# Norm pieces of a finished expert group moved between the second-layer products, on three engines, in a hybrid RWKV and mixture-of-experts layer

## The chip, the cores and the metric

One core of a Trainium2 chip runs the whole layer. The metric is device time in microseconds of one execution. Before the change it was 4061.99 us, the median of three runs (4059.59 to 4078.86).

## What is computed

The input is x, 4096 tokens of 1024 channels, float32. A projection, a pooling mixer, an RWKV-7 recurrence and an output product give `h = LayerNorm(alpha*x + mix)`. Then comes the part that matters here, a two-level mixture of experts and a last norm:

```python
g_top_p, g_idx = lax.top_k(softmax(h @ router_group + b), 1)     # 1 of 4 groups
e_top_logit, e_idx = lax.top_k(logits of that group's 8 experts, 2)
hid = silu(h[tok] @ exp_gate[e]) * (h[tok] @ exp_up[e])          # 1024 -> 256, per expert
ffn[tok] += (hid @ exp_down[e]) * weight                         # 256 -> 1024
y = LayerNorm(alpha * h + ffn) * ln2_g + ln2_b
```

Each token goes to two experts of one group, so a token's sum is complete when its group's eight experts are done.

## The kernel before

Three phases come first (`phase_project`, `phase_rwkv`, `phase_out`); the change leaves them alone. `phase_out` also routes the tokens, writes them to `d_h`, alpha times them to the accumulator `d_acc`, and writes a table of tokens per expert. Experts are ranked by load inside ranked groups, and the r-th expert gets a fixed number of 64-row blocks, `GIVEN[r]`: 7 6 6 5 5 5 5 4, then 6 5 5 5 5 4 4 4, then 7 6 5 4 4 4 4 3, then 4 4 3 3 3 3 3 3. Rows are worked on in spans of 128. The groups have `GGIVEN` = 10, 9, 9, 6 tiles of 128 tokens to norm.

`phase_moe` runs the 32 experts in one unrolled loop with a manual schedule: every engine executes its instructions in the order in which the program emits them, so the place of a call in the text is its place in the queue. All products are float32 split into a high and a low part, three matmuls for each. In expert r:

- `listed` and `load` (L1203, L1228) are DMAs on SP: the token table, and the weights of coming experts into six staging halves `ws`.
- `split` (L1214) turns one staged half into high (ACT copy, L1225) and low (DVE subtraction, L1226). Six halves an expert: g0 g1 u0 u1 d0 d1.
- `hidden` (L1300) is the first layer: for f in 0, 1 the gate and the up product (24 matmuls each, into p_gu banks), then silu (ACT), times (DVE, sg), high part hh (ACT), low part hl (DVE). A dictionary `work` hangs other calls behind the products (f, "g") and (f, "u"), ahead of that f's silu.
- `down` (L1332) is the second layer. A column j is 128 rows by 512 outputs; it has two halves f of three matmuls into one p_y bank. ACT weighs the finished column into y (L1330), and after two columns POOL adds y into `d_acc` by an indirect DMA (`scatter`, L1261).
- Between the columns, `rows` (L1280) prepares the next expert: a turn is four transposes on PE into one m_pt bank (L1275), then ACT writes xh (L1291) and DVE xl (L1292), which frees the bank. After every second turn POOL gathers a coming span of tokens (`ahead`, L1247).
- In the order of before, three columns get their first half, and from then on each column's second half is followed by the first half of the column three places on.

`Norms` handles a finished group while the next group's experts run, in experts i = 1 to 7 of that group. `fetch` gathers one or two tiles of `d_acc` on POOL (L1422). One expert later `stats` runs on DVE behind (0, "g"): sums of each tile (L1378, L1379), then fifteen tiny instructions for the root (`root`, L1382). Behind (1, "g") `apply` makes two DVE passes over each tile (L1406, L1407), and behind (1, "u") `store` writes it out by an indirect DMA on POOL (L1443). The experts before the first finished group, and the first one or two of each group, carry none of this. The last group is normed behind the loop in pairs of tiles, with the root from ACT's log and exponential (`log_root`, L1399). Two loops behind that take overflowing experts and have no passes for these inputs. An indirect DMA keeps its dependence on the POOL DMA just ahead of it, and is freed by hand from those that touch other rows (L1254).

Of the kernel before, what the change touches and what calls it, by code (L numbers as in the profile page):

```python
# [6 lines left out]
F32 = mybir.dt.float32  # L7
# [6 lines left out]
D = 1024  # L14
# [1138 lines left out]
def phase_moe(tc, A, hrow, acc, tab, gtab, plan, out):  # L1153
# [14 lines left out]
    KM = max(GIVEN)  # L1168
    RW = 64 * KM
    with ExitStack() as ctx:  # L1170
        cst = ctx.enter_context(tc.tile_pool(name="m_c", bufs=1))
        wsp = [ctx.enter_context(tc.tile_pool(name=f"m_w{i}", bufs=1)) for i in range(3)]
        wst = ctx.enter_context(tc.tile_pool(name="m_ws", bufs=6))
        xp = ctx.enter_context(tc.tile_pool(name="m_x", bufs=1))
        hp = ctx.enter_context(tc.tile_pool(name="m_h", bufs=1))
        fp = ctx.enter_context(tc.tile_pool(name="m_f", bufs=4))
        sm = ctx.enter_context(tc.tile_pool(name="m_s", bufs=3))
        pg = ctx.enter_context(tc.tile_pool(name="m_pg", bufs=3, space=PSUM))
        py = ctx.enter_context(tc.tile_pool(name="m_py", bufs=3, space=PSUM))
        ptr = ctx.enter_context(tc.tile_pool(name="m_pt", bufs=2, space=PSUM))  # L1180

        manual = ctx.enter_context(ExitStack())
        manual.enter_context(tc.manual_schedule())
# [145 lines left out]

            nc.scalar.activation(y[:n, i * 512:i * 512 + 512], p[:n], AF.Copy, scale=ix[:n, 1:2].bitcast(F32))  # L1330

        def down(r, hid, nxt):  # L1332

            ps = {}
            sp = spans[r]
            hi, lo = W[r]["d"]
            ix = IX.pop(r)
            same = []

            def part(j, f):  # L1340
                b, n = divmod(j, 2)
                a0, a1 = sp[b]
                if f == 0:
                    ps[j] = py.tile([128, 512], F32, name="p_y")
                a, c = hid[f]
                for i, (x, w) in enumerate(((a, hi), (c, hi), (a, lo))):
                    nc.tensor.matmul(ps[j][:a1 - a0], lhsT=x[:, a0:a1], rhs=w[:, f, n * 512:n * 512 + 512],  # L1347
                                     start=f == 0 and i == 0, stop=f == NF - 1 and i == 2)

            J = 2 * len(sp)  # L1350
            left = 2 * len(spans[r + 1]) if r + 1 < NE else 0
            for j in range(3):
                if left:
                    next(nxt)
                    left -= 1
                part(j, 0)
            for j in range(J):
                part(j, 1)
                a0, a1 = sp[j // 2]
                if j % 2 == 0:  # L1360
                    y = hp.tile([128, D], F32, name="y", bufs=4)
                weigh(y, j % 2, ps.pop(j), ix[:, j // 2], a1 - a0)
                if j % 2:
                    same.append(scatter(ix[:, j // 2], y, a1 - a0, r // EG, same))
                if j + 3 < J:
                    part(j + 3, 0)
                for _ in range(-(-left // (J - j))):
                    next(nxt)
                    left -= 1
            for _ in nxt:  # L1370
                pass

        def mean_var(hs):
            st = sm.tile([128, 2, 2, 6], F32, name="f_st")
            mv = sm.tile([128, 2, 2], F32, name="f_mv")
            for i, h in enumerate(hs):
                for c in range(2):
                    nc.vector.bn_stats(st[:, i, c, :], h[:, c * 512:c * 512 + 512])  # L1378
                nc.vector.bn_aggr(mv[:, i, :], st[:, i])  # L1379
            return mv  # L1380

        def root(mv, n):  # L1382

            va = sm.tile([128, 2], F32, name="f_va")[:, :n]
            yi = sm.tile([128, 2], I32, name="f_yi")[:, :n]
            ra = sm.tile([128, 2], F32, name="f_ra")
            tm = sm.tile([128, 2], F32, name="f_tm")[:, :n]
            rs = ra[:, :n]
            nc.vector.tensor_scalar(va, mv[:, :n, 1], 1e-5, None, op0=OP.add)
            nc.vector.tensor_scalar(yi, va.bitcast(I32), 1, None, op0=OP.arith_shift_right)  # L1390
            nc.vector.tensor_scalar(rs.bitcast(I32), yi, -1.0, float(0x5f3759df), op0=OP.mult, op1=OP.add)
            for _ in range(3):
                nc.vector.tensor_tensor(tm, rs, rs, op=OP.mult)
                nc.vector.tensor_tensor(tm, tm, va, op=OP.mult)
                nc.vector.tensor_scalar(tm, tm, -0.5, 1.5, op0=OP.mult, op1=OP.add)
                nc.vector.tensor_tensor(rs, rs, tm, op=OP.mult)
            return ra

        def log_root(mv, n):  # L1399
            ra = sm.tile([128, 2], F32, name="f_ra")  # L1400
            nc.scalar.activation(ra[:, :n], mv[:, :n, 1], AF.Ln, bias=leps)
            nc.scalar.activation(ra[:, :n], ra[:, :n], AF.Exp, scale=-0.5)
            return ra

        def scale(h, mv, rs, i):
            nc.vector.scalar_tensor_tensor(h, h, mv[:, i, 0:1], g2, op0=OP.subtract, op1=OP.mult)  # L1406
            nc.vector.scalar_tensor_tensor(h, h, rs[:, i:i + 1], b2, op0=OP.mult, op1=OP.add)  # L1407

        class Norms:


            def __init__(self, g):
                self.g, self.b, self.got = g, 0, []
                gs = bass.ds(eng.value_load(orow[0:1, g, 1:2], min_val=0, max_val=NG - 1), 1)
                self.ig = sm.tile([128, max(GGIVEN)], I32, name="ig", bufs=2)
                eng.dma_start(self.ig[:, :GGIVEN[g]], tg[gs, :, :GGIVEN[g]].rearrange("g p a -> (g p) a"))

            def fetch(self, n):
                self.new = []
                for _ in range(n):  # L1420
                    h = fp.tile([128, D], F32, name="f_h")
                    ld = nc.gpsimd.indirect_dma_start(  # L1422
# [7 lines left out]
                    self.b += 1  # L1430

            def stats(self, rsqrt):
                if self.got:
                    self.mv = mean_var([h for h, _ in self.got])
                    self.rs = rsqrt(self.mv, len(self.got))

            def apply(self):
                for i, (h, b) in enumerate(self.got):
                    scale(h, self.mv, self.rs, i)

            def store(self):
# [7 lines left out]
                self.got = []  # L1449

        def share(n, k):

# [15 lines left out]
        for r in range(NE):  # L1468
            g, i = divmod(r, EG)
            listed(r + 3)  # L1470
            work = {(0, "g"): [lambda: split(r, "d", 0), lambda: split(r, "d", 1)],
                    (1, "g"): [lambda: split(r + 1, "g", 0), lambda: split(r + 1, "g", 1)],
                    (1, "u"): [lambda: split(r + 1, "u", 0)]}
            if r == 1:
                nc.scalar.dma_start(g2, bcast_row(A["ln2_g"], D))
                nc.scalar.dma_start(b2, bcast_row(A["ln2_b"], D))
                work[0, "u"] = [plan.caps]
            if r == 2:
                work[0, "u"] = [plan.rest]
            if g and i == 1:  # L1480
                norms = Norms(g - 1)
                parts = share(GGIVEN[g - 1], EG - 2) + [0]
            if g and i:
                norms.fetch(parts[i - 1])
# [5 lines left out]
            if norms:  # L1490
                norms.got, norms.new = norms.new, []
            load(r + 1, "d")
            load(r + 2, "gu")
            down(r, hid, rows(r + 1))
        norms = Norms(NG - 1)
        for n in share(GGIVEN[NG - 1], (GGIVEN[NG - 1] + 1) // 2) + [0]:
            norms.fetch(n)
            norms.stats(log_root)
            norms.apply()
            norms.store()  # L1500
            norms.got = norms.new
        manual.close()

        rrow = cst.tile([1, 128, 4], I32, name="rrow")
# [39 lines left out]
        n = nc.values_load(rrow[0:1, 0, 3:4], min_val=0, max_val=S // 128)  # L1544
        av = acc.rearrange("(q p) d -> q p d", p=128)
        ov = o.rearrange("(q p) d -> q p d", p=128)
        with tc.For_i(0, n) as i:
            h = fp.tile([128, D], F32, name="f_h")
            eng.dma_start(h, av[bass.ds(i, 1)].rearrange("q p d -> (q p) d"))
            mv = mean_var([h])  # L1550
            scale(h, mv, log_root(mv, 1), 0)
            eng.dma_start(ov[bass.ds(i, 1)].rearrange("q p d -> (q p) d"), h)


# [46 lines left out]
```

## Time and profile before, and how to read it

| | |
|---|---|
| median of three runs | 4061.99 us |
| the profiled execution, its own time | 4087.32 us |
| its span, first to last instruction | 4085.7 us |
| PE matmul busy | 3409.8 us (83%) |
| DVE busy | 2019.8 us (49%) |
| ACT busy | 1577.1 us (39%) |
| POOL busy | 1628.1 us (40%) |
| mean granted TensorE clock | 0.868 |
| HBM read, written | 324.90, 206.92 MB |

PE is TensorE's matmuls, PEld its weight loads, DVE VectorE, ACT ScalarE, POOL GpSimd, SP the queue of most DMAs. An idle time is put down to the instruction or transfer that ended it. DMA share is the mean busy share of 16 DMA engines. Busy shares are means over stages with different limits, so a stage is read by itself.

### The profile page before, as it was taken

Reading aid. Unit: us, or ns where it says so; the run is one execution under the profiler, and the core shown is the slowest. Engines: PE = TensorE matmul, PEld = TensorE weight load, DVE = VectorE, ACT = ScalarE, POOL = GpSimd, SP = SyncE. Lnnn points to the kernel's source line nnn. Section 1 sums busy time; section 2 is a strip of 40 time slices with the busy share of each in tenths; the row PEclk is TensorE's granted clock in tenths of the full one; section 3 lists DMA queues with packets and bytes.
Section 4 is the critical chain, followed back from the end, with each engine's and each line's share of the span. In section 5 each row is a group of like instructions: output and inputs, shape, how many; then the busy total and the mean of one; then the engine's idle time right before and its main releaser. Section 6 shows DMA issues by size and latency. Waiting matters only on the chain. (4 is left out here: it accounts for less than half of the span.)

```text
span 4085.7 us, 70444 instructions
## 1 busy us (share of the span) xinstructions
PE 3409.8 (83%) x27401; PEld 2825.9 (69%) x27401; DVE 2019.8 (49%) x4087; ACT 1577.1 (39%) x2672; POOL 1628.1 (40%) x2951
## 2 busy tenths in 40 slices
PE   7999999999668888878888868999668887777772
PEld 6878877777557777767776756777557776566652
DVE  3222222222447776767666635565544445455564
ACT  2222211111244545454545435565424443333432
POOL 3000120000177777777777731334322223222222
PEclk9999999999777878787878769999879998887876
DMA  7433333322223333333333325565357777677763
GB/s 245 173 137 151 147 129 129 116 99 85 80 58 84 71 84 72 78 73 81 77 73 80 68 70 194 140 154 142 85 149 188 197 199 208 184 190 209 214 194 92
DMA packets 509752, 531.20 MB, mean 130 GB/s; under 512 B 297854, under 2 KB 411688, under 8 KB 505321
## 3 DMA queue, kind: packets, MB, share of 16 engines
q1 hardware_dynamic: 445752, 367.94, 31.7%
q0 software_dynamic: 33920, 106.02, 10.8%
q10 hardware_dynamic: 29744, 52.73, 3.5%
q8 instruction: 216, 3.54, 0.4%
q14 instruction: 120, 0.98, 0.1%
HBM read 324.90 MB, written 206.92 MB: 130 GB/s over the span
## 5 line engine op out<-in xcount | busy, mean ns | idle before, releaser
L134 PE MATMUL acc<-xhi,wh 128*128 128x512 f32 x1408 | 565.9, 402 | 5.4 <-DVE zo L176 5.1
L135 PE MATMUL acc<-xlo,wh 128*128 128x512 f32 x1408 | 559.4, 397 | 0.0
L136 PE MATMUL acc<-xhi,wl 128*128 128x512 f32 x1408 | 559.3, 397 | 0.0
L491 POOL TENSOR_TENSOR db<-db,tmp 96x126 f32<-96x126 f32 (+22 forms) x992 | 449.8, 453 | 77.7
L489 POOL TENSOR_TENSOR tmp<-db,gi 96x126 f32<-96x126 f32 (+22 forms) x992 | 430.6, 434 | 77.7
L176 DVE SCALAR_TENSOR_TENSOR zo<-acc,omu,zm 128x512 f32<-128x512 f32 x160 | 120.0, 751 | 660.5 <-ACT zm L173 622.3
L173 ACT ACTIVATE zm<-acc,muc 128x512 f32<-128x512 f32 x160 | 110.1, 690 | 719.7 <-PE acc L136 718.4
L134 PEld LDWEIGHTS acc<-xhi,wh 128*128 128x128 f32 x1408 | 265.4, 189 | 72.0 <-DVE zo L176 5.4
L135 PEld LDWEIGHTS acc<-xlo,wh 128*128 128x128 f32 x1408 | 265.7, 189 | 66.4 <-issue 3.8
L136 PEld LDWEIGHTS acc<-xhi,wl 128*128 128x128 f32 x1408 | 265.5, 189 | 63.4
L174 POOL COPY carry<-zm 128x1 f32<-128x1 f32 x160 | 30.4, 191 | 664.4 <-ACT zm L173 664.4
L1275 PE MATMUL m_pt<-m_id,xg 128*128 128x128 f32 (+1 forms) x648 | 108.9, 300 | 198.1 <-DVE xl L1292 163.7
L1275 PEld LDWEIGHTS m_pt<-m_id,xg 128*128 128x128 f32 (+1 forms) x648 | 83.3, 160 | 236.5 <-DVE xl L1292 179.1
L1261 POOL DMA_INDIRECT d_acc<-y,ix x81 | 131.8, 1627 | 266.3 <-DMA d_acc<-y,ix 107.1
L1061 PE MATMUL o_ps<-owh,mh 128*128 128x512 f32 x512 | 212.4, 415 | 17.1 <-ACT owh L889 17.0
L1347 PE MATMUL p_y<-wh_d,hh 128*128 128x512 f32 (+1 forms) x324 | 169.4, 523 | 59.2 <-ACT y L1330 51.4
L1292 DVE TENSOR_TENSOR xl<-m_pt,xh 128x512 fp32r<-128x512 f32 (+1 forms) x162 | 99.3, 629 | 240.0 <-ACT xh L1291 213.8
L1247 POOL DMA_INDIRECT xg<-d_h,ix x81 | 78.3, 966 | 337.9 <-PE m_pt L1275 328.9
L1061 PE MATMUL o_ps<-owh,ml 128*128 128x512 f32 x512 | 207.1, 404 | 5.2 <-POOL ml L876 5.2
L1061 PE MATMUL o_ps<-owl,mh 128*128 128x512 f32 x512 | 205.3, 402 | 0.5 <-DVE owl L890 0.3
L445 DVE TENSOR_TENSOR g<-tr,mask 128x384 f32<-128x384 f32 x256 | 130.4, 550 | 142.9 <-PE tr L443 142.9
L443 PE MATMUL tr<-ar,kb 64*128 64x128 f32 x1536 | 178.9, 364 | 24.9 <-DVE kb L430 17.0
(352 smaller groups left out, 8802.7 us busy)
## 6 DMA issues: line engine op xcount, KB each, us to landing
d_rkv<-zo SPq DMA_DIRECT2D x144, 256.0 KB
ws<-in_exp_gate_dram SPq DMA_DIRECT2D x64, 512.0 KB
ws<-in_exp_up_dram SPq DMA_DIRECT2D x64, 512.0 KB
ws<-in_exp_down_dram SPq DMA_DIRECT2D x64, 512.0 KB
xq<-in_x_dram SPq DMA_DIRECT2D x32, 512.0 KB
d_xsp<-xhi ACTq DMA_DIRECT2D x8, 2048.0 KB
d_xsp<-xlo ACTq DMA_DIRECT2D x8, 2048.0 KB
xlo<-d_xsp SPq DMA_DIRECT2D x8, 2048.0 KB
```

Of the source, the lines that this page charges most:

```text
L134: nc.tensor.matmul(ps, lhsT=whi[i][:, k, :], rhs=xhi[:, k, :], start=k == 0, stop=False)
L135: nc.tensor.matmul(ps, lhsT=whi[i][:, k, :], rhs=xlo[:, k, :], start=False, stop=False)
L136: nc.tensor.matmul(ps, lhsT=wlo[i][:, k, :], rhs=xhi[:, k, :], start=False, stop=k == KD - 1)
L176: nc.vector.scalar_tensor_tensor(zo, ps, omu[:, ix:ix + 1], zm[:, :SEG], op0=OP.mult, op1=OP.add)
L443: nc.tensor.matmul(ps[h][:, p, :], lhsT=KB[hs, i, :], rhs=AR[hs, i, :], start=True, stop=True)
L445: nc.vector.tensor_tensor(G[:, h, c::NC, :], ps[h], masks[c % 2].unsqueeze(1).to_broadcast([128, 3, 128]), op=OP.mult)
L489: e.tensor_tensor(tm, Dh[:, :a, x:x + 1].to_broadcast([96, a, b]), G[:, x, x + 1:].unsqueeze(1).to_broadcast([96, a, b]), op=OP.mult)
L491: e.tensor_tensor(Dh[:, :a, x + 1:], Dh[:, :a, x + 1:], tm, op=OP.add)
L1061: nc.tensor.matmul(ps, lhsT=a[:, k, :], rhs=w[k][:, ns], start=k == 0 and i == 0, stop=k == KD - 1 and i == 2)
L1261: st = nc.gpsimd.indirect_dma_start(out=acc, out_offset=bass.IndirectOffsetOnAxis(ap=ix[:n, 0:1], axis=0), in_=y[:n], in_offset=None, boun ...
L1275: nc.tensor.transpose(pt[:, k, :n], xg[:n, (4 * i + k) * 128:(4 * i + k + 1) * 128], ident[:n, :n])
L1347: nc.tensor.matmul(ps[j][:a1 - a0], lhsT=x[:, a0:a1], rhs=w[:, f, n * 512:n * 512 + 512], start=f == 0 and i == 0, stop=f == NF - 1 and i ...
```

## The change

The pools of staging memory come first, p_y loses one PSUM bank and m_pt gains it. A norm pass is split in three: x * root - mean * root on ACT, times ln2_g on DVE, plus ln2_b on POOL. `stats` returns a list of small pieces, and `down` issues one of them around each half column from the third on, in the expert that fetched the tile; scale, product and store follow in the next expert's first layer. In `down` each column is now finished at once, and the turns stand ahead of the half columns, as early as they come. Three splits move a place ahead. The last group is normed tile by tile, with four tiles fetched up front.

```diff
+        wst = ctx.enter_context(tc.tile_pool(name="m_ws", bufs=6))
+        wsp = [ctx.enter_context(tc.tile_pool(name=f"m_w{i}", bufs=1)) for i in range(3)]
         cst = ctx.enter_context(tc.tile_pool(name="m_c", bufs=1))
-        wsp = [ctx.enter_context(tc.tile_pool(name=f"m_w{i}", bufs=1)) for i in range(3)]
-        wst = ctx.enter_context(tc.tile_pool(name="m_ws", bufs=6))
...
-        py = ctx.enter_context(tc.tile_pool(name="m_py", bufs=3, space=PSUM))
-        ptr = ctx.enter_context(tc.tile_pool(name="m_pt", bufs=2, space=PSUM))
+        py = ctx.enter_context(tc.tile_pool(name="m_py", bufs=2, space=PSUM))
+        ptr = ctx.enter_context(tc.tile_pool(name="m_pt", bufs=3, space=PSUM))
...
-        def down(r, hid, nxt):
+        def down(r, hid, nxt, extra):
...
+                if f == 0:
+                    return
+                if n == 0:
+                    y[b] = hp.tile([128, D], F32, name="y", bufs=4)
+                weigh(y[b], n, ps.pop(j), ix[:, b], a1 - a0)
+                if n:
+                    same.append(scatter(ix[:, b], y[b], a1 - a0, r // EG, same))
             J = 2 * len(sp)
+            todo = [(0, 0), (1, 0), (0, 1), (1, 1)] + [(j, f) for j in range(2, J) for f in range(NF)]
             left = 2 * len(spans[r + 1]) if r + 1 < NE else 0
-            for j in range(3):
-                if left:
+            extra = list(extra)
+            for i, (j, f) in enumerate(todo):
+                for _ in range(-(-left // max(1, len(todo) - 3 - i))):
                     next(nxt)
                     left -= 1
-                part(j, 0)
-            for j in range(J):
-                part(j, 1)
...
+                    if extra and i > 1:
+                        extra.pop(0)()
+                part(j, f)
+                if extra and i > 1:
+                    extra.pop(0)()
...
             def stats(self, rsqrt):
-                if self.got:
-                    self.mv = mean_var([h for h, _ in self.got])
-                    self.rs = rsqrt(self.mv, len(self.got))
+                self.got, self.new = self.new, []
...
+                def shift():
+                    nc.vector.scalar_tensor_tensor(mr[:, :n], mv[:, :n, 0], -1.0, ra[:, :n], op0=OP.mult, op1=OP.mult)
+                return ([lambda i=i, h=h: sums_of(i, h) for i, (h, _) in enumerate(self.got)]
+                        + rsqrt(mv, ra, n) + [shift])
+            def scale(self, only=None):
+                for i, (h, b) in enumerate(self.got):
+                    nc.scalar.activation(h, h, AF.Identity, bias=self.mr[:, i:i + 1], scale=self.ra[:, i:i + 1])
             def apply(self):
                 for i, (h, b) in enumerate(self.got):
-                    scale(h, self.mv, self.rs, i)
+                    nc.vector.tensor_tensor(h, h, g2, op=OP.mult)
             def store(self):
                 for h, b in self.got:
+                    nc.gpsimd.tensor_tensor(h, h, b2, op=OP.add)
                     st = nc.gpsimd.indirect_dma_start(
...
             work = {(0, "g"): [lambda: split(r, "d", 0), lambda: split(r, "d", 1)],
-                    (1, "g"): [lambda: split(r + 1, "g", 0), lambda: split(r + 1, "g", 1)],
-                    (1, "u"): [lambda: split(r + 1, "u", 0)]}
+                    (0, "u"): [lambda: split(r + 1, "g", 0)],
+                    (1, "g"): [lambda: split(r + 1, "g", 1), lambda: split(r + 1, "u", 0)],
+                    (1, "u"): [lambda: split(r + 1, "u", 1)]}
...
-                work[0, "g"].append(lambda: norms.stats(root))
-                work[1, "g"].append(norms.apply)
-                work[1, "u"].append(norms.store)
+                work[0, "g"] += [norms.scale, norms.apply]
+                work[0, "u"].append(norms.store)
             hid = hidden(r, work)
-            split(r + 1, "u", 1)
...
+            if g and i:
+                extra = norms.stats(root)
+            down(r, hid, rows(r + 1), extra)
         norms = Norms(NG - 1)
-        for n in share(GGIVEN[NG - 1], (GGIVEN[NG - 1] + 1) // 2) + [0]:
...
+        norms.fetch(min(4, GGIVEN[-1]))
+        every = norms.new
+        while every or norms.b < GGIVEN[-1]:
+            norms.new = every[:1]
+            every = every[1:]
+            for x in norms.stats(log_root):
+                x()
+            norms.scale()
+            norms.apply()
+            norms.store()
+            if norms.b < GGIVEN[-1]:
+                norms.fetch(1)
+                every += norms.new
```

The root's instructions are the same, cut into one opening piece of three and three steps of four; `log_root` is one piece. The overflow loop behind uses the same three passes.

## Rows read from the trace of the kernel before

**Rows 1.** Windows by stage: length, busy PE, PEld, DVE, ACT, POOL, clock, DMA share, GB/s.

```profile
2997.00:3323.90 326.90, 279.35 (x1553) 237.30 (x1553) 145.00 (x263) 146.28 (x219) 76.76 (x60) 0.97 0.69 183
3323.90:3531.10 207.20, 151.77 (x885) 129.99 (x883) 125.20 (x231) 80.43 (x123) 64.71 (x49) 0.86 0.72 203
3531.10:3805.60 274.50, 210.76 (x1154) 178.36 (x1153) 143.15 (x252) 104.66 (x157) 76.02 (x58) 0.82 0.70 192
3805.60:4023.90 218.30, 164.04 (x1073) 136.29 (x1071) 127.38 (x239) 87.03 (x137) 63.56 (x46) 0.85 0.67 183
```

**Rows 2.** Waits of the expert loop: who waited for whom, us, times, longest.

```profile
PE m_pt L1275 <- DVE xl L1292: 161.8, 31, 10.7
...
PE p_y L1347 <- ACT y L1330: 51.4, 66, 0.8
```

**Rows 3.** Windows of single experts, columns as in rows 1: 4, 7, 20, 21, 25, 27.

```profile
3148.30:3178.60 30.30, 26.28 (x158) 21.97 (x157) 12.49 (x16) 14.37 (x23) 7.48 (x7) 1.00 0.73 190
3238.00:3260.50 22.50, 20.15 (x146) 18.18 (x145) 12.06 (x15) 13.02 (x21) 7.18 (x5) 1.00 0.73 203
...
3682.50:3710.00 27.50, 20.55 (x137) 18.47 (x136) 17.44 (x34) 12.01 (x19) 7.70 (x8) 0.88 0.83 239
3710.00:3744.10 34.10, 22.85 (x137) 20.06 (x137) 21.68 (x39) 12.10 (x19) 10.30 (x8) 0.75 0.68 190
3827.20:3848.90 21.70, 19.33 (x138) 17.15 (x137) 10.83 (x14) 11.67 (x19) 6.13 (x6) 1.00 0.91 251
3877.70:3911.20 33.50, 22.04 (x138) 17.72 (x137) 20.64 (x39) 11.46 (x19) 10.05 (x8) 0.75 0.67 195
```

**Rows 4.** Timeline of PE in expert 4's second layer: start, us, instruction, idle before.

```profile
3166.47 0.66 PE L1275 MATMUL m_pt<-m_id,xg 128*128 128x128 f32 x4 [1.69 <-DVE xl L1292]
...
3167.90 0.39 PE L1347 MATMUL p_y<-wh_d,hl 128*128 128x512 f32 x1
3168.13 0.40 PE L1347 MATMUL p_y<-wl_d,hh 128*128 128x512 f32 x1
3169.30 0.50 PE L1347 MATMUL p_y<-wh_d,hh 128*128 128x512 f32 x1 [0.78 <-ACT y L1330]
```

**Rows 5.** Lines of the expert loop: group, count, busy us, mean ns, idle before.

```profile
L1226 DVE TENSOR_TENSOR wl_g<-ws,wh_g 128x1024 fp32r<-128x1024 f32 x62 | 73.2, 1222 | 15.1 <-ACT wh_g L1225 15.1
...
L1225 ACT ACTIVATE wh_g<-ws 128x1024 fp32r<-128x1024 f32 x62 | 61.8, 1044 | 0.0
...
L1406 DVE SCALAR_TENSOR_TENSOR f_h<-f_h,f_mv,g 128x1024 f32<-128x1024 f32 x28 | 35.8, 1279 | 0.0
```

**Rows 6.** Timeline in phase_out: a POOL subtraction and a DVE pass begun beside it.

```profile
2493.33 2.40 POOL L876 TENSOR_TENSOR ml<-m,mh 128x1024 fp32r<-128x1024 f32 x1 [9.29 <-ACT mh L875]
...
2493.84 2.97 DVE L1145 SCALAR_TENSOR_TENSOR h<-h,ln_mv,g 128x1024 f32<-128x1024 f32 x1
```

**Rows 7.** Timeline of POOL, experts 19 and 20: a second scatter, then the norm gather.

```profile
3688.57 1.59 POOL L1261 DMA_INDIRECT d_acc<-y,ix  x1 [5.24 <-DMA d_acc<-y,ix]
3696.01 1.22 POOL L1422 DMA_INDIRECT f_h<-d_acc,ig  x1 [5.85 <-DMA d_acc<-y,ix]
```

**Rows 8.** Timelines behind the loop: POOL's first gather and last store, DVE, ACT.

```profile
4034.46 0.99 POOL L1422 DMA_INDIRECT f_h<-d_acc,ig  x1 [2.29 <-DMA d_acc<-y,ix]
...
4038.91 1.28 DVE L1378 BATCH_NORM_STATS2 f_st<-f_h 128x6 f32<-128x512 f32 x2 [21.91 <-DMA f_h<-d_acc,ig]
4040.23 0.21 DVE L1379 BATCH_NORM_AGGREGATE f_mv<-f_st 128x2 f32<-128x12 f32 x1
...
4044.10 1.28 ACT L1402 ACT_TABLE_LOAD   x1
4045.39 0.20 ACT L1402 ACTIVATE f_ra<-f_ra 128x2 f32<-128x2 f32 x1
...
4074.01 0.98 POOL L1443 DMA_INDIRECT out_dram<-f_h,ig  x1 [3.11 <-DMA out_dram<-f_h,ig]
```

**Rows 9.** Timelines ahead of the loop: the last split of first weights, the first turn.

```profile
2965.41 1.06 ACT L1225 ACTIVATE wh_u<-ws 128x1024 fp32r<-128x1024 f32 x1 [0.71 <-DMA ws<-in_exp_up_dram]
...
2987.96 1.94 PE L1275 MATMUL m_pt<-m_id,xg 128*128 128x128 f32 x8 [34.48 <-DMA ws<-in_exp_up_dram]
```

More of the change, by code (lines that the diff above doesn't have):

```diff
@@ L1370, in down @@
             for _ in nxt:
                 pass
[L1373 to L1407, printed above, removed]
+            for x in extra:
+                x()
@@ L1432, in stats, with sums_of @@
             def stats(self, rsqrt):
-                if self.got:
-                    self.mv = mean_var([h for h, _ in self.got])
-                    self.rs = rsqrt(self.mv, len(self.got))
+                self.got, self.new = self.new, []
+                n = len(self.got)
+                if not n:
+                    return []
+                st = sm.tile([128, 2, 2, 6], F32, name="f_st")
+                mv = sm.tile([128, 2, 2], F32, name="f_mv")
+                ra = sm.tile([128, 2], F32, name="f_ra")
+                mr = sm.tile([128, 2], F32, name="f_mr")
+                self.ra, self.mr = ra, mr
+                def sums_of(i, h):
+                    for c in range(2):
+                        nc.vector.bn_stats(st[:, i, c, :], h[:, c * 512:c * 512 + 512])
+                    nc.vector.bn_aggr(mv[:, i, :], st[:, i])
+                def shift():
[5 more added lines that the diff above has]
+                    nc.scalar.activation(h, h, AF.Identity, bias=self.mr[:, i:i + 1], scale=self.ra[:, i:i + 1])
             def apply(self):
                 for i, (h, b) in enumerate(self.got):
-                    scale(h, self.mv, self.rs, i)
+                    nc.vector.tensor_tensor(h, h, g2, op=OP.mult)
             def store(self):
                 for h, b in self.got:
+                    nc.gpsimd.tensor_tensor(h, h, b2, op=OP.add)
                     st = nc.gpsimd.indirect_dma_start(
@@ L1449, in store, with root, begin, step @@
                 self.got = []
+        def root(mv, ra, n):
+            va = sm.tile([128, 2], F32, name="f_va")[:, :n]
+            yi = sm.tile([128, 2], I32, name="f_yi")[:, :n]
+            tm = sm.tile([128, 2], F32, name="f_tm")[:, :n]
+            rs = ra[:, :n]
+            def begin():
+                nc.vector.tensor_scalar(va, mv[:, :n, 1], 1e-5, None, op0=OP.add)
+                nc.vector.tensor_scalar(yi, va.bitcast(I32), 1, None, op0=OP.arith_shift_right)
+                nc.vector.tensor_scalar(rs.bitcast(I32), yi, -1.0, float(0x5f3759df), op0=OP.mult, op1=OP.add)
+            def step():
+                nc.vector.tensor_tensor(tm, rs, rs, op=OP.mult)
+                nc.vector.tensor_tensor(tm, tm, va, op=OP.mult)
+                nc.vector.tensor_scalar(tm, tm, -0.5, 1.5, op0=OP.mult, op1=OP.add)
+                nc.vector.tensor_tensor(rs, rs, tm, op=OP.mult)
+            return [begin, step, step, step]
+        def log_root(mv, ra, n):
+            def both():
+                nc.scalar.activation(ra[:, :n], mv[:, :n, 1], AF.Ln, bias=leps)
+                nc.scalar.activation(ra[:, :n], ra[:, :n], AF.Exp, scale=-0.5)
+            return [both]
         def share(n, k):
@@ L1476, in phase_moe @@
                 nc.scalar.dma_start(b2, bcast_row(A["ln2_b"], D))
-                work[0, "u"] = [plan.caps]
+                work[0, "u"].append(plan.caps)
             if r == 2:
[L1479 to L1482, printed above, removed]
+                work[0, "u"].append(plan.rest)
+            extra = []
             if g and i:
+                if i == 1:
+                    norms = Norms(g - 1)
+                    parts = share(GGIVEN[g - 1], EG - 2) + [0]
                 norms.fetch(parts[i - 1])
-                work[0, "g"].append(lambda: norms.stats(root))
-                work[1, "g"].append(norms.apply)
-                work[1, "u"].append(norms.store)
+                work[0, "g"] += [norms.scale, norms.apply]
+                work[0, "u"].append(norms.store)
             hid = hidden(r, work)
-            split(r + 1, "u", 1)
-            if norms:
-                norms.got, norms.new = norms.new, []
             load(r + 1, "d")
             load(r + 2, "gu")
-            down(r, hid, rows(r + 1))
+            if g and i:
+                extra = norms.stats(root)
+            down(r, hid, rows(r + 1), extra)
         norms = Norms(NG - 1)
-        for n in share(GGIVEN[NG - 1], (GGIVEN[NG - 1] + 1) // 2) + [0]:
-            norms.fetch(n)
-            norms.stats(log_root)
+        norms.fetch(min(4, GGIVEN[-1]))
[4 more added lines that the diff above has]
+            for x in norms.stats(log_root):
+                x()
+            norms.scale()
             norms.apply()
             norms.store()
-            norms.got = norms.new
+            if norms.b < GGIVEN[-1]:
+                norms.fetch(1)
+                every += norms.new
         manual.close()
@@ L1546, in phase_moe @@
         ov = o.rearrange("(q p) d -> q p d", p=128)
+        again = norms
         with tc.For_i(0, n) as i:
@@ L1549, in phase_moe @@
             eng.dma_start(h, av[bass.ds(i, 1)].rearrange("q p d -> (q p) d"))
-            mv = mean_var([h])
-            scale(h, mv, log_root(mv, 1), 0)
+            again.new = [(h, None)]
+            for x in again.stats(log_root):
+                x()
+            again.scale()
+            again.apply()
+            nc.gpsimd.tensor_tensor(h, h, b2, op=OP.add)
             eng.dma_start(ov[bass.ds(i, 1)].rearrange("q p d -> (q p) d"), h)
```

15 lines of the change are left out of this document (2 added, 13 removed).

## The prediction

> **What bounds the kernel now.** I read the stretches by stage first [rows 1]. The expert loop runs from 2997.0 to 4023.9 us, and the change touches that loop and the 61.8 us behind it, up to the span's 4085.7; the 2997 us ahead of it stay. No engine is full in the loop: PE is busy 279 + 152 + 211 + 164 = 806 of 1026.9 us, DVE 541, and the transfers take 0.67 to 0.72 of their engines. So the loop is made of waits, and the waits of its stretch say which [rows 2]: PE stood 161.8 us in 31 places before a turn (four transposes into one m_pt bank) until DVE had written xl and so freed a bank, and 51.4 us in 66 places before a product of the second layer, until ACT had emptied a p_y bank.
>
> Where they lie is seen by setting experts of one size beside each other [rows 3]. Expert 25 (three blocks, no norm piece yet) takes 21.7 us, expert 27 (the same size, two tiles normed) 33.5. DVE's busy time doubles, 10.83 to 20.64; ACT's hardly moves. PE's busy time rises by 2.7 because the granted clock averaged 0.75 instead of 1.00 (2.4 GHz, and 1.2 GHz after PE stood still); the other 9.1 us are idle PE. Experts 7 and 21, of four blocks, show the same: 22.5 and 34.1. DVE is 64% busy in expert 21 and still ends last, because of its order: the norm's sums and passes stand in the first layer, ahead of sg, hl and the first xl, so they push the next expert's turns back, and while the second layer runs DVE has little to do.
>
> Experts without norm pieces wait too [rows 4]: the third turn stands 1.69 us until xl frees one of two banks, and the fourth second-layer column starts 1.17 us after the matmul before it instead of the usual 0.23, so each such wait of 0.78 costs 0.94.
>
> **The change part by part.**
>
> Order of the second layer, and a p_y bank given to turns. Now every column is finished at once (its two halves, then weigh). A bank is asked for again one column later: behind the end of a column lie a column's three remaining matmuls and a turn (0.69 + 0.36 = 1.05 us), more than the 0.94 that a weigh needs, so I count these waits as gone, with 0.3 us an expert left. With three m_pt banks the fourth turn is the first to wait for xl, 3.2 us into the second layer; the xl that the third turn awaited now has one split of 1.22 us [rows 5] fewer ahead of it, so it comes at about 4.1 - 1.2 = 2.9. I count that wait as gone as well. Expert 4 gains 3 x 0.94 + 1.9 = 4.7; the first ten experts together about 44.
>
> Splits moved (g0, u0 and u1 each a place earlier): no work added. DVE is busy 12 of 30 us where no norm runs [rows 3], so there is room, and in norm experts their time is inside the period below. Each split frees its staging buffer, so SP issues the loads behind it a little earlier; nothing on SP waits longer.
>
> Norm pieces. Per tile DVE loses two passes of 1.28 [rows 5] and gains one product of 1024 columns, like a split, 1.22; a pass gains one tiny shift (0.2). ACT gains a scale pass: a plain copy of that size takes 1.04, twice that bounds the per-row scale and bias above, I take 1.2, being nearest to the copy; ACT is busy 12 of 34 us [rows 3], so it is covered unless the shift comes late. POOL gains an add of 1024 columns: 2.40 by the subtraction of the same shape [rows 6]. What that costs DVE is shown there too: a pass of two SBUF inputs that began while POOL's subtraction ran took 2.97 instead of 1.28, ending 1.07 after POOL. So an add holds DVE for 0 to 2.4 us; I take 2.97 - 1.28 = 1.7.
>
> The Trainium skill, "SBUF — State Buffer", section "SBUF: two separate sides", calls the shared VectorE and GpSimd port an exclusive lock, kept for the whole instruction. The trace agrees that the pass waits, with 1.7 in [rows 6]. By that rule the 28 adds in the loop could cost DVE 28 x 2.4 = 67 us, where the row's price gives 28 x 1.7 = 48.
>
> So with two tiles DVE needs before's busy time - 5.1 + 2.4 + 0.2 + 3.4 = before + 0.9: 22.6 in expert 21, 21.6 in expert 27; with one tile 18.0 in expert 20. The sums now run during the second layer, where DVE was idle, and the shift, scale and product follow early in the next first layer. DVE's order then has few holes; for hand-overs from ACT (hh twice, the first scale, splits) I add 2.5. The periods are 25 us for two tiles and four blocks, 24 with three blocks, 20.5 with one. PE alone needs 22.5 - 2.7 = 19.8 [expert 7 less its waits], so DVE sets the two-tile period, and PE still waits some 4 us there.
>
> What is queued behind the new waits: on DVE the turns' xl stand behind a sum that waits for its gathered tile; on ACT silu and hh behind a scale that waits for the shift; on POOL the token gathers and scatters behind an add that waits for DVE's product. POOL has a chain of its own [rows 7]: an expert's second scatter stood 5.2 us until the first had landed, and the gather of norm rows started 7.4 after the second. With two stores (8.6, by 2 x 2.4 of adds and a store's landing), two token gathers (2.5) and its scatters it needs about 25 us a two-tile expert: level with DVE, not above.
>
> Transfers. Experts shrink, bytes don't. Busy share times length is 226, 149, 192 and 146 us in the four stretches [rows 1]; expert 25 ran at 0.91 without a stall [rows 3], and nothing here shows more. So stretch two can't go below 149 / 0.91 = 164 and stretch three below 211.
>
> Sum, stretch by stretch. First ten experts: 326.9 - 44 = 283. Experts 10 to 15: three of five blocks at 26 to 28 (PE 30.3 - 4.7 = 25.6; DVE 25 and two more xl), then 20.5, 25, 26: 153, raised to 164 by the transfers; gain 43. Experts 16 to 23: 34.5 and 29 for the large two (against 25.6, a block adds 96 matmuls of 64 columns at 2.4 GHz, 2.6, a fourth pair of columns 2.8, the clock 0.9), 26, then 25, 20.5, 25, 20.5, 23.5: 204, raised to 211; gain 63. Experts 24 to 31: two at 21.7, three at 20, two at 24, the last at 22: 173; gain 45. Together 44 + 43 + 63 + 45 = 195. I take 10 off for clock still lost after waits of 4 us: 185.
>
> The end. The first sums started at 4038.91 and the last store was issued at 4074.01 [rows 8], six tiles in pairs; the first four gathers are issued together before and after. Now a tile is a chain: sums 1.5, log and exponential some 0.2 each, a table load of 1.28 between them, shift 0.2, scale 1.2, product 1.2: 5.8 a tile, because the next tile's sums stand behind the product on DVE. Six tiles 35, a first table load and the last add 3.7, hops 1.5: 40 instead of 35.1, a loss of 5 (0 to 10).
>
> Staging memory first: nothing. The first weights were split by 2966.5 and PE took up the first turn only at 2987.96 [rows 9], behind routing; 20 us of slack cover it either way.
>
> Net 180 us. The profiled execution took 4087.3 us, 25 over the median of 4061.99; I set the gain against the median: **3880**.
>
> **The rivals.** (a) DVE stays the bound by more: adds hold it for all of 2.4 us, and waits of 4 to 6 us in every norm expert keep the clock low. Price: 28 x 0.7 = 20, and about 2.5 us of low clock in 17 experts, 42, of which 10 are counted: 52, so 3930. For it: rows 6; against it: part of the adds will fall beside xl, which has one operand in PSUM, and no row shows such an instruction held. 0.18. (b) Transfers bind below 0.91, at 0.85 say: the loop can't go under 713 / 0.85 = 839, which is what I forecast, but stretches two and three rise to 175 and 226, 26 more: 3905. 0.12. (c) The new bank split doesn't do what it says: two p_y banks keep the 66 waits, 62 us: 3940. Against it: the 1.05 of cover. 0.05. (d) Slower: the norm gather lands after DVE has come to its sums. It was issued 13.5 us into expert 20 [rows 7] and at the end the first use came 4.5 after the issue [rows 8], so 18 us in; DVE is there at 14 to 17. One to four us late costs little, since PE still has six columns to do. If POOL's chain stretches by 12 us (each landing doubles), the sums, the xl behind them and the next first layer all wait, 17 experts take some 37 us and PE runs at half clock: 17 x 6 = 100 lost instead of 151 won, 4062 - 44 + 100 + 5 = 4123. It decides from a gather 10 us later than DVE. 0.05. (e) The unseen gains hold (no clock loss, no transfer floor): 3855 or below, down to 3830. Part of my forecast.
>
> **How the numbers follow.** Forecast 0.60 (3815 to 3920), rivals (a) 0.18, (b) 0.12, (c) 0.05, (d) 0.05. The range 3815 to 3955 leaves out (d), the worst of (a) and (c) and the best cases. A measurement of this kernel can tell about 0.5%, 20 us, from no change: faster 0.92, same 0.03, slower 0.05.
>
> **What would show it.** Right: waits for p_y near zero; turns no longer waiting in the first ten experts (about 25.7 us where expert 4 took 30.3); two-tile experts at 24 to 26; transfer share near 0.9; DVE passes stretched to 3 us beside POOL's adds; the end a few us longer. Wrong: sums that wait on the gather, splits that wait on weights, or norm experts still above 29 us.

## The result, and the profile after

The changed kernel takes 3921.59 us (median of four runs, 3913.39 to 3925.03), 0.964 of the time before (95% interval 0.961 to 0.967; with a fourth run the kernel before has a median of 4065.01). Forecast: 3880, range 3815 to 3955. Its profiled execution took 3922.84 us, span 3921.2.

Stretches of the changed kernel, cut as in [rows 1]: the first ten experts, 10 to 15, 16 to 23, 24 to 31, and what lies behind the loop. Columns: stretch, its length, busy us (and instructions) of PE, PEld, DVE, ACT, POOL, then granted clock, DMA share, GB/s.

```profile
2984.00:3258.40 274.40, 267.81 (x1552) 238.64 (x1553) 147.33 (x276) 145.06 (x219) 77.05 (x60) 0.98 0.81 217
3258.40:3437.90 179.50, 143.07 (x886) 125.90 (x885) 112.02 (x216) 90.83 (x132) 85.84 (x60) 0.90 0.79 238
3437.90:3669.40 231.50, 190.86 (x1153) 170.39 (x1152) 134.96 (x248) 113.88 (x165) 94.06 (x65) 0.91 0.78 226
3669.40:3854.00 184.60, 158.09 (x1073) 135.68 (x1071) 125.90 (x236) 95.72 (x146) 80.62 (x54) 0.93 0.75 215
3854.00:3921.20 67.20, 0.00 (x0) 0.00 (x0) 18.27 (x30) 26.48 (x31) 27.17 (x19) 0.54 0.31 99
```

The loop went from 1026.9 to 870.0 us, the end from 61.8 to 67.2. By stretch the loop gained 52.5, 27.7, 43.0 and 33.7 us: more than forecast in the first ten experts (44), less in the others (43, 63, 45). In this execution the loop also began 13 us earlier; that is not the change's, since in the profiled executions of this study it began between 2975 and 3003.

Waits of the loop (engine, line, what was waited for: us in total, times, longest us):

```profile
DVE f_st L1413 <- DMA f_h<-d_acc,ig: 107.7, 25, 15.6
...
PE p_gu L1314 <- DVE xl L1293: 72.5, 13, 15.3
PE p_y L1349 <- ACT hh L1324: 15.0, 8, 5.5
PE p_y L1349 <- DVE hl L1325: 10.2, 7, 2.7
PE m_pt L1276 <- DMA xg<-d_h,ix: 9.1, 1, 9.1
PE m_pt L1276 <- DVE xl L1293: 2.9, 1, 2.9
```

Of the two waits of [rows 2], the turns' 161.8 us are down to 2.9, and p_y's wait for ACT to empty a bank is gone from PE's list. A new one stands in their place: PE's first layer waits 72.5 us for xl, and DVE 107.7 us for gathered norm tiles. Expert 29 shows how they hang together; its neighbours 28 and 30 took 20.3 and 18.3 us, it took 36.7. The timelines of POOL, then DVE, then PE (start, us, engine, line, operation, what ended the idle time before):

```profile
3765.70 2.57 POOL L1262 DMA_INDIRECT d_acc<-y,ix  x1 [0.31 <-ACT wh_g L1226]
3776.51 1.43 POOL L1262 DMA_INDIRECT d_acc<-y,ix  x1 [8.23 <-ACT xh L1292]
3781.63 0.99 POOL L1389 DMA_INDIRECT f_h<-d_acc,ig  x1 [3.69 <-DMA d_acc<-y,ix]
...
3774.28 1.62 DVE L1293 TENSOR_TENSOR xl<-m_pt,xh 128x512 fp32r<-128x512 f32 x3
3785.92 1.29 DVE L1413 BATCH_NORM_STATS2 f_st<-f_h 128x6 f32<-128x512 f32 x2 [10.02 <-DMA f_h<-d_acc,ig]
...
3789.72 0.37 DVE L1293 TENSOR_TENSOR xl<-m_pt,xh 128x256 fp32r<-128x256 f32 x1
...
3790.14 0.53 PE L1314 MATMUL p_gu<-xl,wh_g 128*128 128x192 f32 x1 [9.55 <-DVE xl L1293]
```

Both scatters are still expert 27's, whose products had ended at 3758.7, so POOL ran most of an expert behind PE. The second scatter starts 10.8 us after the first, and expert 28's norm gather 5.1 us behind that. DVE has stood 10 us before the sums, and the last xl, 0.37 us of work, is behind them, so PE stands too. Where the releaser named had long been done (ACT's xh before the second scatter), I read a wait for the first scatter's landing; the run with the scatters apart, below, tests it.

### The profile page after: what moved, and what is told of

The parts are those of the page before. It is cut to its first block, busy times and chain, and to the rows that moved or that the text cites. A ratio compares the mean times of both kernels' runs of the same rounds, so it can differ in the third digit from the quotient of the medians.

```text
span 3921.2 us, 70586 instructions
## 1 busy us (share of the span) xinstructions
PE 3350.2 (85%) x27401; PEld 2801.9 (71%) x27401; DVE 1999.1 (51%) x4077; ACT 1620.8 (41%) x2718; POOL 1696.2 (43%) x2985
## 3 DMA queue, kind: packets, MB, share of 16 engines
q0 software_dynamic: 33920, 106.02, 10.8%
## 5 line engine op out<-in xcount | busy, mean ns | idle before, releaser
L1314 PE MATMUL p_gu<-xl,wh_g 128*128 128x256 f32 (+4 forms) x512 | 159.2, 311 | 72.5 <-DVE xl L1293 72.5
L443 PE MATMUL tr<-ar,kb 64*128 64x128 f32 x1536 | 178.5, 364 | 25.5 <-DVE kb L430 17.4
L443 PEld LDWEIGHTS tr<-ar,kb 64*128 64x128 f32 x1536 | 147.3, 252 | 46.5 <-DVE g L445 17.3
L370 ACT ACTIVATE thw<-tr,chans 128x256 f32<-128x256 f32 x96 | 45.6, 475 | 297.6 <-PE tr L369 263.8
L1349 PE MATMUL p_y<-wh_d,hh 128*128 128x512 f32 (+1 forms) x324 | 145.5, 449 | 15.0 <-ACT hh L1324 15.0
L1314 PE MATMUL p_gu<-xh,wh_u 128*128 128x256 f32 (+4 forms) x512 | 157.9, 308 | 0.0
```

The costliest lines, as they stand in the source:

```text
L443: nc.tensor.matmul(ps[h][:, p, :], lhsT=KB[hs, i, :], rhs=AR[hs, i, :], start=True, stop=True)
L1314: nc.tensor.matmul(p[:, :N], lhsT=a[:, k, fs], rhs=c[:, k, :N], start=k == 0 and i == 0, stop=k == KD - 1 and i == 2)
```

## The experiments

"Loop" is from the first product of expert 0 to the last of the second layer, "end" the rest of the span. Ratios are to the kernel before on the same chip, whose median was 4065 to 4087 us from chip to chip. Loop and end are read from one profiled execution of each version. How far such loops differ by themselves is seen from versions with the same work in the same places: with the staging pools put back the loop is 5.8 us longer than the change's, and that of "store later" 6.0 us longer than that of "early and apart". So a few us of loop show nothing, and where ratio and loop disagree both are given.

| run | ratio (95%) | loop | end |
|---|---|---|---|
| before | 1 | 1026.9 | 61.8 |
| the change | 0.964 (0.961 to 0.967) | 870.0 | 67.2 |
| order alone | 0.968 (0.964 to 0.971) | 883.8 | 59.2 |
| banks back | 0.970 (0.965 to 0.974) | 888.6 | 65.6 |
| DVE passes | 0.960 (0.956 to 0.963) | 866.5 | 57.4 |
| staging back | 0.964 (0.961 to 0.967) | 875.8 | 66.8 |
| end in pairs | 0.966 (0.962 to 0.969) | 868.5 | 66.8 |
| early gather | 0.958 (0.954 to 0.963) | 838.7 | 80.9 |
| scatters apart | 0.954 (0.951 to 0.957) | 826.9 | 65.7 |
| early and apart | 0.946 (0.944 to 0.949) | 790.6 | 67.5 |
| early and apart, no adds | 0.940 (0.937 to 0.943) | 764.8 | 68.5 |
| early and apart, DVE passes | 0.941 (0.937 to 0.945) | 773.2 | 57.6 |
| early and apart, store later | 0.943 (0.940 to 0.946) | 796.6 | 57.5 |
| order alone, apart | 0.961 (0.958 to 0.965) | 875.8 | 58.8 |

**The order alone.** The old `Norms`, stages and passes, with the new `down`, banks and splits.

> The kernel before with the new column order, banks, turns and splits, and with the norm work where it was (DVE passes, sums in the next expert's first layer). The first ten experts as in the changed kernel, 274 us instead of 327 in all theories. Theory 1: moving the norm work won little because the gathers came late, so this is near the changed kernel, 3920 to 3965 us. Rival: the move of the norm pieces carries the gain in the later 22 experts as forecast, and without it they stay near their old lengths less 3 us each: 3950 to 4000.

0.968, and 271.1 us for the first ten experts. All of the gain there comes from the order, the banks and the three splits that moved. What the norm pieces add is 883.8 - 870.0 = 14 us of loop, less 8 us at the end: the first theory's reading. The intervals of the two ratios overlap, so it is not shown that in the changed kernel the pieces gained anything.

**The bank split undone.**

```diff
-        py = ... name="m_py", bufs=2
-        ptr = ... name="m_pt", bufs=3
+        py = ... name="m_py", bufs=3
+        ptr = ... name="m_pt", bufs=2
```

> Three banks for p_y and two for turns, all else as changed. If the third turn bank matters as forecast (1.7 us of wait in each expert without norm pieces), the first ten experts are 12 to 20 us longer and the whole 3935 to 3950; if the new order alone does it, 3915 to 3925.

The loop is 18.6 us longer (by the ratio, 0.970, the interval just overlaps the change's), the first ten experts 9.2 (283.7 against 274.5), not 12 to 20. An expert of five blocks without norm work takes 25.7 instead of 25.4, where before the change it took 30.3: there the order did the work, together with the moved splits, which no run tests alone. The bank pays where norm sums hold xl back, a wait that was 2.9 us in the changed kernel:

```profile
PE m_pt L1276 <- DVE xl L1293: 46.0, 25, 5.8
```

**Passes back on DVE**, in the changed kernel's places, and no scale on ACT or add on POOL.

```diff
-                    nc.scalar.activation(h, h, AF.Identity, bias=self.mr[...], scale=self.ra[...])
+                    nc.vector.scalar_tensor_tensor(h, h, self.mv[:, i, 0:1], g2, op0=OP.subtract, op1=OP.mult)
...
-                    nc.vector.tensor_tensor(h, h, g2, op=OP.mult)
+                    nc.vector.scalar_tensor_tensor(h, h, self.ra[:, i:i + 1], b2, op0=OP.mult, op1=OP.add)
...
-                    nc.gpsimd.tensor_tensor(h, h, b2, op=OP.add)
```

> The norm passes as two DVE passes again, no scale on ACT and no add on POOL, in the changed kernel's places. By the prediction's prices (2 x 1.28 against 1.22 + 1.7 of hold) no change, 3910 to 3930. Theory 1: POOL loses 2.4 us a tile ahead of its scatters and of the next gather, so gathers come earlier and it gains 10 to 40: 3880 to 3910. Rival: the three-engine split is worth its DVE time, 1.3 a tile, and without it the kernel takes 3935 to 3960.

By the ratio, no difference from the change (the intervals overlap). The loop is the same within 4 us and the end 10 us shorter. The three-engine pass bought nothing in the loop. Starts of the sums behind the loop, first of the change, then of this run, show why the end is shorter:

```profile
3873.10 1.28 DVE L1413 BATCH_NORM_STATS2 f_st<-f_h 128x6 f32<-128x512 f32 x2
3879.16 1.28 DVE L1413 BATCH_NORM_STATS2 f_st<-f_h 128x6 f32<-128x512 f32 x2
```

```profile
3887.42 1.28 DVE L1413 BATCH_NORM_STATS2 f_st<-f_h 128x6 f32<-128x512 f32 x2
3892.02 1.28 DVE L1413 BATCH_NORM_STATS2 f_st<-f_h 128x6 f32<-128x512 f32 x2
```

A tile takes 6.1 us against 4.6. The first DVE pass needs only the mean and runs while ACT makes the root; the pass on ACT needs the root first.

**Staging pools last; the end in pairs.**

> The staging pools placed last as before the change, all else as changed. Forecast: no difference from the changed kernel, 3910 to 3930 us (the changed kernel's ratio was 0.964). If the first weights' loads matter, the first expert starts later and it takes 5 to 15 more.

> The last group's tiles in pairs behind the loop, on three engines as changed. The prediction's chain has one tile's sums behind the other's product; in pairs two tiles share the root's chain, so the end takes 35 to 40 us of work instead of 41 and the 67.2 us behind the loop become 61 to 66: 3912 to 3920 us. If the three-engine pass itself makes the end long, 66 to 70 and no gain.

Neither differs from the change: 0.964 with the pools last, as forecast, and for the pairs an end of 66.8 against 67.2, so the three-engine pass makes the end long, not the single tiles.

**Early gather.** The next expert's norm tiles are fetched behind the first gather of tokens in `down`.

```diff
                     if i:
                         ahead()
+                        if hook:
+                            hook.pop()()
...
-                norms.fetch(parts[i - 1])
+                hook.append(lambda n=parts[i]: norms.fetch(n))
```

> The gather of norm tiles is issued one expert earlier, behind the first gather of tokens. Theory 1 (the changed kernel loses time where a norm gather stands on POOL's queue behind two scatters and their landings, so that DVE's sums wait and the xl behind them stop the next first layer): the 107.7 us that DVE waits for these gathers go, the idle PE ahead of first layers (72.6 us in experts 11 to 29) nearly goes, and with the low clock behind it: 3820 to 3850 us. Theory 2 (POOL's own length, adds and landings, or the adds' hold on DVE, is the bound): the wait moves to another place and the time stays at 3900 to 3925. Theory 3 (transfers bind): not under 3870.

The first theory's waits went (PE before the first layer: 72.5 to 4.7 us), its time hardly did: 0.958, an interval that overlaps the change's. Another wait took the place, turns for their token gathers, and the end grew by 14 us, because POOL's last scatter was issued 18.7 us behind PE's last product instead of 4.9. PE's waits, then POOL's timeline of this run:

```profile
PE m_pt L1276 <- DMA xg<-d_h,ix: 47.8, 9, 12.5
```

```profile
3731.68 2.60 POOL L1262 DMA_INDIRECT d_acc<-y,ix  x1 [0.30 <-ACT sg L1323]
3743.93 1.68 POOL L1262 DMA_INDIRECT d_acc<-y,ix  x1 [9.65 <-issue]
3745.16 2.86 POOL L1435 TENSOR_TENSOR f_h<-f_h,b 128x1024 f32<-128x1024 f32 x1
...
3755.00 1.87 POOL L1248 DMA_INDIRECT xg<-d_h,ix  x1 [0.30 <-DMA ws<-in_exp_down_dram]
```

Two scatters in a row stand 12 us apart. POOL's round (what it issues for one expert, with the landings it waits for) looks too long by itself. That is the second theory's case, and it called for its own test.

**Scatters apart.** One token gather is kept back behind each scatter but the last, so that the POOL DMA ahead of the second scatter is not the first.

```diff
-                    if i:
+                    if i and b < len(spans[r]) - kept:
                         ahead()
...
                     same.append(scatter(ix[:, b], y[b], a1 - a0, r // EG, same))
+                    if b < kept(r):
+                        ahead()
```

where `kept(r)` is one less than the smaller number of spans of experts r and r + 1. The two scatters touch different rows, and of such DMAs the kernel keeps the dependence only on the one just ahead on POOL's queue, so the second need not wait for the first any more. It was run on the changed kernel alone, and together with the early gather, which there stands ahead of the first token gather:

> The changed kernel with one gather of tokens kept back behind each scatter of an expert, so that two scatters are not neighbours on POOL's queue and the second need not wait for the first to land; the norm gather stays where the change has it. Theory 2 as it now stands (two scatters in a row, the second 10 to 12 us behind the first, make POOL's round longer than PE's, whatever is behind it): norm gathers come some 10 us earlier in experts with two scatters, most of the 107.7 us of DVE waits go, 3860 to 3900 us. Theory 1 alone (the norm gather's place behind the last scatter's landing): that wait stays, 3905 to 3925. Transfers as the bound: no gain, 3910 to 3930.

> Both: the norm gather one expert earlier and ahead of a gather of tokens, and the scatters kept apart. If POOL's chain of landings is what holds the loop, the experts fall to what PE needs (25.4 for five blocks, 18 to 20 for three and four): loop 740 to 790 us instead of 839 with the early gather alone, 3820 to 3870 in all. If transfers bind at a share of 0.91, the loop can't go under some 750 to 780 and the share of the last three stretches shows 0.9. If scatters take their 10 us for another reason than the neighbour, no change against the early gather alone, 3905 to 3925.

0.954 apart, as the second theory had it, and 0.946 together; the early gather alone had 0.958. Apart alone cut DVE's wait for norm gathers in the loop from 107.7 to 51.1 us and PE's wait for xl from 72.5 to 32.0. The two add up: the loop falls by 31 us with the early gather, by 43 with the scatters apart and by 79 with both. That they do more together than the sum isn't shown; the 5 us between are within what loops differ by. Stretches two to four of the two together:

```profile
3262.30:3420.40 158.10, 141.25 (x886) 124.47 (x885) 126.17 (x209) 90.17 (x132) 90.93 (x59) 0.95 0.88 267
3420.40:3619.10 198.70, 186.24 (x1154) 164.28 (x1153) 147.03 (x248) 113.13 (x165) 100.21 (x65) 0.97 0.88 261
3619.10:3780.60 161.50, 150.31 (x1073) 129.72 (x1071) 132.09 (x236) 95.55 (x145) 87.07 (x55) 0.98 0.81 247
```

Two-tile experts of three and four blocks now take 24 to 28 us (14, 19, 21, 23, 27, 29: 27.8, 25.1, 24.8, 25.3, 23.9, 25.3; 15, ahead of seven blocks, 33.7; 31, the last, which prepares no next expert, 18.4) and one-tile ones 18 to 20. Now POOL's adds show, in expert 29 of this run (rows of POOL and DVE):

```profile
3723.54 3.30 POOL L1441 TENSOR_TENSOR f_h<-f_h,b 128x1024 f32<-128x1024 f32 x1 [3.72 <-DVE f_h L1437]
3724.51 3.41 DVE L1227 TENSOR_TENSOR wl_g<-ws,wh_g 128x1024 fp32r<-128x1024 f32 x1
...
3728.62 2.82 DVE L1328 TENSOR_TENSOR hl<-sg,hh 128x192 fp32r<-128x192 f32 x1 [0.43 <-ACT hh L1327]
3728.83 2.38 POOL L1441 TENSOR_TENSOR f_h<-f_h,b 128x1024 f32<-128x1024 f32 x1
3731.36 1.21 DVE L1227 TENSOR_TENSOR wl_g<-ws,wh_g 128x1024 fp32r<-128x1024 f32 x1
```

The split takes 3.41 beside the add and 1.21 without it; hl takes 2.82 instead of 0.36.

**The adds.** Three runs on top of "early and apart": the addition of ln2_b left out in the loop; two DVE passes as above; the adds and stores emitted behind the first layer, with DVE passes behind the loop.

> Early norm gather and scatters apart, and inside the loop the addition of ln2_b on POOL left out (behind the loop it stays), to price POOL's adds. With the early gather and scatters apart DVE passes beside the adds were stretched by about 60 us in all and PE waited 31 us for products of the second layer. If the adds' hold is what keeps two-tile experts at 24 to 25 us, they fall to 20 to 22 and the loop from 791 to 760 to 772 us. If DVE's own work sets them, 785 to 791.

> Early norm gather and scatters apart, with the norm passes as two DVE passes again, in the loop and behind it. A tile costs DVE 1.3 us more of its own and no add holds it. If holds are near 2 us each, two-tile experts gain about 1.5 us and the loop is 772 to 786; if holds cost nothing that counts, two-tile experts lose 2.6 us and the loop is 805 to 815. Behind the loop 57 to 59 us instead of 67.5, as in the run with DVE passes. In all 3825 to 3842 or 3855 to 3870.

> Early norm gather and scatters apart, the adds and stores moved behind the first layer, so that they run beside xl and the sums, which no row shows held; behind the loop two DVE passes a tile. If the adds hold only passes with two SBUF inputs, two-tile experts fall to 21 to 23 us and the loop to 765 to 780, the end to 57 to 59: 3815 to 3832. If POOL's longer round then makes token gathers late, turns wait and the loop is 790 to 810: 3840 to 3860.

Without adds the loop falls by 26 us, and experts 23, 27 and 29 to 19. Leaving the adds out also shortens POOL's round, so PE's waits have to tell which of the two counted. First "early and apart", then the same without adds:

```profile
PE p_y L1356 <- ACT hh L1327: 27.1, 15, 6.4
PE p_y L1356 <- DVE hl L1328: 12.2, 7, 2.4
...
PE m_pt L1276 <- DMA xg<-d_h,ix: 3.3, 1, 3.3
```

```profile
PE m_pt L1276 <- DMA xg<-d_h,ix: 20.8, 4, 8.9
PE p_y L1356 <- ACT hh L1327: 10.6, 6, 5.7
```

The waits for hl and for hh (which stands behind DVE's sg) fell from 39.3 to 10.6 us, and the one wait on POOL, for token gathers, rose. So it was the hold that set the two-tile experts. The gain isn't even: experts 15 and 22 grew to 41.0 and 27.2 us, where turns waited for their token gathers. With DVE passes the loop falls by 17, and the end by 10: 3825.44 us, the fastest version that computes everything. The third forecast was missed: POOL has no other work between the old place and the new one, so its order stayed, the adds ran beside the same passes and only the end gained.

**Order alone, apart.** Was POOL's round the limit with the norm work in its old place too?

> The new column order, banks, turns and splits with the norm work where it was before the change (the run of the order alone, loop 884 us), and the scatters kept apart as in the other runs. There the gather has an expert's time to land, and DVE's passes and sums in the first layer set the norm experts (24 to 33 us). If so, a shorter round on POOL brings little: loop 865 to 884, 3935 to 3960 us, and the norm pieces between the columns are worth the 100 us that lie between this and 773, once POOL's round is short. Rival: POOL's round held these experts too, then the loop falls to 800 to 840 and the place of the norm pieces is worth 30 to 60.

Hardly: the loop is 875.8, 8 us less, where the rival had 44 to 84. By the ratio the gain is larger, 0.968 to 0.961, some 25 us with intervals that just overlap, and 3909.58 us is below the 3935 to 3960 forecast. What PE waits for stayed, hh behind DVE's sums and passes. First the order alone, then with the scatters apart:

```profile
PE p_y L1348 <- ACT hh L1323: 94.6, 21, 7.6
```

```profile
PE p_y L1352 <- ACT hh L1323: 91.5, 20, 7.5
```

So the place of the norm pieces is worth 883.8 - 866.5 = 17 us of loop (both with DVE passes) while POOL's round is long, and 875.8 - 773.2 = 103 with scatters apart and the early gather that this place needs. The sizes are rough: by the ratios of whole times the two are 0.008 and 0.020, some 32 and 83 us.

## Why the prediction was right, and where it was off

It was right in sign and range, 42 us too low. In the profiled executions the loop lost 156.9 us where 185 were forecast, and that makes 28 of the 42; the rest lies between profiles and medians, since the profiled execution of before, from whose rows the forecast was worked out, was 25 us above the median. In part it was luck that the miss stayed so small: the first ten experts gained 8.5 us more than forecast, the 10 us taken off for the clock came in useful, and both covered part of the 46.6 us that the later stretches fell short. By its steps:

- **Order and banks**: forecast 44 us in the first ten experts, measured 52.5. Expert 4 went from 30.3 to 25.4, as worked out; the surplus came mostly from experts 0 and 1, which gained 7.4 us each. That the order, with the moved splits, frees the third turn was right; the extra bank does so only in part, as its own run shows (25.7 without it).
- **The norm pieces**: the step that failed is POOL's round, "level with DVE, not above". I priced it with the scatters of [rows 7] (5.2 us of idle time, 6.8 from start to start) and with a norm gather issued 13.5 us into the expert and of use 18 us in. In the changed kernel the gather was issued 21.1 us into its expert (13.0 before; medians of 18 experts), and the first sums began 25.5 us in. Neighbouring scatters of one expert, in experts 10 to 31, stood 7.2 us apart before and 9.4 after, from start to start (medians of 23 each), and the norm gather had moved from an expert's lead to none. That the scatters' landings grew because the same transfers now ran in less time is likely, but no run tests it. That is rival (d) in small: I gave it 0.05 as one big case, where it came as 72.5 us of idle PE. "One to four us late costs little" overlooked that the last xl stands behind the sums, and that a late first layer makes the next scatters late.
- **DVE's period**: the pair of experts 25 and 27, set side by side as one size, isn't one: 25 has four blocks and 27 three (`GIVEN`). The other pair, 7 and 21, is of one size and says the same. The periods of 24 to 25 us for two tiles were met in five of six such experts once the gathers were in time; one tile, forecast at 20.5, took 18 to 20. Before that the adds' hold hardly counted: DVE passes beside the loop's 28 adds were stretched by some 19 us in the changed kernel and by some 53 with early and apart, 1.9 an add against the 1.7 I took. The price of rival (a) was fair, its place was hidden behind the gathers.
- **Transfers**: the floors of 164 and 211 us do not hold; the version with DVE passes ran these stretches in 150.1 and 193.4, the first at a share of 0.92.

```profile
3259.50:3409.60 150.10, 139.78 (x885) 123.24 (x884) 119.35 (x214) 79.10 (x122) 65.56 (x49) 0.95 0.92 281
3409.60:3603.00 193.40, 184.19 (x1153) 163.39 (x1152) 139.94 (x251) 103.11 (x156) 75.89 (x55) 0.98 0.89 266
```

- **The end**: +5 forecast, +5.4 measured, by the chain of one tile (6.1 us against my 5.8). **Staging**: nothing, as forecast.
- **Rivals (b) and (c)** did not come: shares stayed at 0.75 to 0.79 in the later stretches, and PE no longer waited for p_y to be emptied.

The Trainium skill, "SBUF — State Buffer", section "SBUF: two separate sides", limits the lock between VectorE and GpSimd to VectorE instructions with two SBUF inputs (or a 2-port mode). The runs agree: with early and apart, 18 of the 20 splits and subtractions hl (two SBUF inputs) that began while an add ran took at least 0.3 us longer, while in the changed kernel none of the 13 xl that began beside an add, which read one operand from PSUM, and none of the 13 BATCH_NORM_STATS2 instructions, which have one SBUF input, did. It also goes the other way: an add that began behind a running product of DVE took 3.3 us instead of 2.4.

## What to carry to other kernels

Before work is moved to an earlier place, follow the queue that feeds it through a whole round, and count each landing that it waits for at the length that it has under the denser traffic to come. Where the program keeps a DMA's dependence on its neighbour, as this kernel does, two scatters in a row cost a landing; an unrelated gather between them took it away here. To lift that dependence outright was not tried. Splitting a pass over three engines pays only if the helper's span does not fall beside VectorE passes with two SBUF inputs, and if no value is needed sooner than before.

## What was not expected

Busy share times length of the transfers is not a constant of the work: stretch two had 0.72 x 207.2 = 149 us before and 0.92 x 150.1 = 138 in the fastest version, stretch three 192 and 172, for the same weights and tokens (42 MB in stretch two in both). A floor worked out from a slower run was too high by a tenth. Why the busy time shrinks stays open.
